# Moving the value-weight loads, the rope tables and the folded output-weight stores of a decoder trunk kernel

## The chip, the cores and the metric

The kernel runs on one core of one Trainium2 chip. The metric is the device time of one execution in microseconds (us). The kernel before has a median of 2416.42 us over 3 runs (2415.17 to 2416.45).

## The reference

One layer of a decoder trunk on 2048 tokens of width 1024, all in fp32, with 256 memory tokens:

```python
h = rmsnorm(x, mix_norm_g)
q, k, v, g, u = split(h @ w_in)                    # 5 x 512 columns
y_ret = silu(g) * head_rmsnorm(retention(q, k, v, positions))   # 4 heads, rotary q and k
y_pool = pool_mixer(u, pool_w, pool_scale)         # 4 groups: window mean minus token, then a 128x128 matrix
x = x + concat([y_ret, y_pool]) @ w_out
x = x + cross_attn(rmsnorm(x), mem_n, xa_wq, xa_wkv, xa_wo)     # 4 heads of 256, memory of 256
x = x + conv_glu_ffn(rmsnorm(x), ...)              # width 2816, causal conv of 3
return rmsnorm(x)
```

## The kernel before, in words

**Arithmetic.** Every fp32 product is done as three matmuls of rounded operands. `split` (lines 256 to 267) makes the two halves of an operand: the high half is an ACT activation (L259, or L262 with a scale per partition), the low half is a DVE subtraction (L243 or L251). `passes` (269 to 273) issues the three matmuls: high by high (L271), high by low (L272), low by high (L273). A matmul therefore first waits for ACT, and its two companions for DVE.

**Tokens.** They go through in two blocks of T = 1024 (b = 0 and 1), each in two stretches of SUB = 512. P is 128, KT is 8 tiles of the model width, HEADS is 4, NMEM is 256.

**Weights folded at the start.** A generator, `folded_weights` (439), runs once and is advanced step by step by `folded(n)` (2010). Its steps in order: keys and values of the memory; for each of four heads the key side is multiplied into the query weight `wqT`, evacuated at L548 and stored to `Md`; then each pooling matrix is multiplied into its rows of the output weight, evacuated at L592 and stored to `WPd` (L594); then for each head and each half of the columns, a "half item", the memory values are multiplied into `wo`, evacuated at L633 and stored to `VWd` (L634). There are eight half items. A loop over n (2021 to 2036) advances this generator once per n and interleaves token loads. At n = 16 to 19 it also calls `value_weights` (730), which loads 512 KB of `w_v` and splits it; this stands ahead of the step of the generator, so that the load is issued ahead of the rows of `wqT` that the step loads.

**After that,** for each block: `values` (739) multiplies tokens by the split value weights and calls `between` after every half, which advances partial sums of tokens and, from its third call on, the tables of the rotary embedding (`rope_steps`, 1998, which stores them by SP at L2005). Then come the projections of the heads, two steps of the generator, and what is left of the work behind, with one step of the generator after each. Then the output units (L2116 on): for each of 8 tiles of the model width, unit n loads a half of `wout_r` (L2118) and a half of `WPd` (L2119) into one slot, splits both (`pairs`) and multiplies them with the mixed tokens. Between the first units the generator is advanced by (1, 2, 4, 0, ...) steps.

**Places.** Tiles come from fixed arenas: `raws` has five 4 KB places for arriving weights (R three, S two), `prs` places for split pairs (Q, and what other arenas lend), Z eight places of 4 KB for evacuated results, TT for temporaries. A slot that is taken again makes its new writer wait for its last reader; a store that still reads a Z slot holds up the next evacuation into it. PSUM has five banks for matmul results (`mm`), so a sixth result waits until the first was evacuated.

**Order.** The program is put into each engine's queue by a scheduler that follows the order in which the code issues, with a look ahead; where the code says `issue_after` or `keep_in_program_order`, it is bound. On each engine instructions run in that order, so an instruction that waits holds all behind it. SP issues nearly all loads, ACT the stores named above.

## Time and profile before

| what | value |
|---|---|
| median of 3 runs | 2416.42 us |
| profiled execution | 2421.08 us, span 2419.3 us |
| granted clock of PE in it | 0.997 |
| busy: PE, DVE, ACT, POOL | 2390.1, 1734.0, 1350.3, 276.0 us |
| DMA | 511.53 MB, mean 211 GB/s |

The span runs from the first to the last instruction of the core. A row of a timeline gives the start in us, the duration of one instruction (or of a merged group, from first start to last end), the engine, the line and the operation with the names of what it writes and reads; in brackets stands the time that its engine was idle just before it, and what ended that. A matmul of 128x512 is listed with 0.39 us, but the next one starts 0.23 us later, since they overlap. An engine's name with a q (SPq, ACTq) is its issuing of DMAs, whose transfers run on 16 DMA engines. In the rows by stretch, the columns are the stretch, its length, the busy time (and instructions) of PE, its weight loads, DVE, ACT and POOL, the granted clock of PE, the share of time that the DMA engines are busy, and GB/s.

### The profile page before, as it was taken

To read this page: it belongs to the slowest core of one execution; us is meant where nothing else is said; L and a number is where in the kernel's file an instruction comes from. 1 tells how busy PE (TensorE), PEld (TensorE's weight loads), DVE (VectorE), ACT (ScalarE), POOL (GpSimd) and SP (SyncE) were. 2 spreads that over 40 slices of the span, in tenths; PEclk is the share of its full clock that TensorE was granted. 3 is DMA by queue.
4 is the path that set the end of the run, shared out by engine and by line. 5 is a ranking of instruction groups with operands and counts; after the bars stand their busy time and mean duration, and the time that the engine had idled before them with its cause. 6 is when DMAs were issued, how large, how long until landed. Compare 5 with 4: busy or idle time off the path is not lost.

```text
span 2419.3 us, 33286 instructions
## 1 busy us (share of the span) xinstructions
PE 2390.1 (99%) x11186; PEld 1993.0 (82%) x11186; DVE 1734.0 (72%) x2904; ACT 1350.3 (56%) x2488; POOL 276.0 (11%) x437
## 2 busy tenths in 40 slices
PE   9999999999999999999999999999999999999998
PEld 8888878888888888888888888888888888887886
DVE  7787774754667665665789776987677698877876
ACT  7654564443445543434555555755555577676673
POOL 0010000063034444100001000110000000000000
PEclk9999999999999999999999999999999999999999
DMA  9732187499688799785477554765455479757952
GB/s 360 262 122 90 63 269 231 135 255 329 194 231 218 188 244 322 195 283 191 140 243 258 184 190 131 251 194 183 158 175 185 134 257 314 238 178 265 345 180 74
DMA packets 267451, 511.53 MB, mean 211 GB/s; under 512 B 29184, under 2 KB 58384, under 8 KB 267280
## 3 DMA queue, kind: packets, MB, share of 16 engines
q1 hardware_dynamic: 209312, 402.30, 50.1%
q0 software_dynamic: 32768, 77.61, 13.1%
q10 hardware_dynamic: 25200, 29.49, 3.5%
q8 instruction: 88, 1.44, 0.2%
q14 instruction: 83, 0.68, 0.1%
HBM read 397.61 MB, written 180.89 MB: 239 GB/s over the span
## 4 chain that ended last, share of the span: by engine, by line
PE 94%; DMA 2%; ACT 2%; DVE 1%; issue 0%; SPq 0%; ACTq 0%; DVEq 0%
PE mm L271 29%; PE mm L272 29%; PE mm L273 29%; PE aux L271 1%; PE aux L273 1%; PE aux L272 1%; ACT G L259 1%; PE aux L901 1%; DMA WPd<-Z 1%; PE aux L778 1%; DVE Z L243 1%; PE aux L806 1%; PE aux L790 0%; PE aux L808 0%; DMA R<-wkv 0%
## 5 line engine op out<-in xcount | busy, mean ns | idle before, releaser
L271 PE MATMUL mm<-G,Q 128*128 128x512 f32 (+1 forms) x1631 | 624.7, 384 | 6.9 <-ACT Q L259 2.7
L273 PE MATMUL mm<-G,Q 128*128 128x512 f32 (+1 forms) x1631 | 619.8, 383 | 0.8 <-DVE Q L243 0.8
L272 PE MATMUL mm<-G,Q 128*128 128x512 f32 (+1 forms) x1503 | 574.1, 382 | 0.2 <-DVE G L251 0.2
L272 PE MATMUL mm<-G,E 128*128 128x512 f32 (+1 forms) x1092 | 420.7, 385 | 0.0
L271 PE MATMUL mm<-G,E 128*128 128x512 f32 (+1 forms) x1092 | 419.2, 386 | 0.5 <-ACT E L259 0.5
L273 PE MATMUL mm<-G,E 128*128 128x512 f32 (+1 forms) x1092 | 418.4, 385 | 0.4 <-DVE E L243 0.4
L271 PEld LDWEIGHTS mm<-G,Q 128*128 128x128 f32 x1631 | 307.0, 188 | 69.2 <-ACT Q L259 4.0
L273 PEld LDWEIGHTS mm<-G,Q 128*128 128x128 f32 x1631 | 306.8, 188 | 60.6 <-DVE Q L243 1.8
L272 PEld LDWEIGHTS mm<-G,Q 128*128 128x128 f32 x1503 | 283.0, 188 | 53.5 <-DVE G L251 0.4
L243 DVE TENSOR_TENSOR Z<-Z,mm 128x512 f32<-128x512 f32 (+1 forms) x322 | 216.4, 676 | 124.6 <-PE mm L273 121.8
L251 DVE SCALAR_TENSOR_TENSOR Z<-Z,vecs 128x1024 f32<-128x1024 f32 x176 | 224.9, 1282 | 50.3 <-ACT Z L1134 48.0
L271 PEld LDWEIGHTS mm<-G,E 128*128 128x128 f32 x1092 | 205.3, 188 | 41.8 <-ACT E L259 0.7
L273 PEld LDWEIGHTS mm<-G,E 128*128 128x128 f32 x1092 | 205.3, 188 | 41.8 <-DVE E L243 0.7
L272 PEld LDWEIGHTS mm<-G,E 128*128 128x128 f32 x1092 | 205.3, 188 | 41.0
L1071 ACT ACTIVATE E<-R 128x512 fp32r<-128x512 f32 (+1 forms) x165 | 101.6, 616 | 146.9 <-PE mm L272 138.7
L243 DVE TENSOR_TENSOR Q<-R,Q 128x512 fp32r<-128x512 f32 x174 | 119.0, 688 | 53.0 <-ACT Q L259 34.7
L243 DVE TENSOR_TENSOR T<-T 128x512 f32<-128x512 f32 (+4 forms) x189 | 130.0, 692 | 23.4 <-ACT T L432 12.0
L243 DVE TENSOR_TENSOR G<-T,G 128x512 fp32r<-128x512 f32 (+1 forms) x173 | 113.8, 678 | 32.4 <-ACT G L1018 18.9
L1018 ACT ACTIVATE G<-T 128x512 fp32r<-128x512 f32 x186 | 111.8, 623 | 36.5 <-DMA T<-Gd 28.6
L1134 ACT ACTIVATE Z<-Z,vecs 128x1024 f32<-128x1024 f32 x88 | 109.2, 1242 | 31.8 <-DVE Z L243 30.8
L1071 ACT ACTIVATE E<-S 128x512 fp32r<-128x512 f32 (+1 forms) x107 | 65.9, 616 | 108.8 <-PE mm L272 106.9
L243 DVE TENSOR_TENSOR E<-R,E 128x512 fp32r<-128x512 f32 (+1 forms) x133 | 89.3, 675 | 43.8 <-ACT E L1071 43.1
(348 smaller groups left out, 3948.3 us busy)
## 6 DMA issues: line engine op xcount, KB each, us to landing
T<-Gd SPq DMA_DIRECT2D x173, 256.0 KB, 4.3
Ud<-w_up POOLq DMA_DIRECT2D x132, 256.0 KB, 9.1
Gd<-Z SPq DMA_DIRECT2D x110, 256.0 KB, 2.6
R<-Ud SPq DMA_DIRECT2D x106, 256.0 KB, 2.8
R<-w_up SPq DMA_DIRECT2D x80, 256.0 KB, 3.1
S<-Ud SPq DMA_DIRECT2D x70, 256.0 KB, 2.9
Gd<-T SPq DMA_DIRECT2D x56, 256.0 KB, 3.3
S<-w_up SPq DMA_DIRECT2D x52, 256.0 KB, 3.1
```

Source lines behind the costliest of these rows:

```text
L243: return eng.tensor_tensor(out=out, in0=a, in1=b, op=op)
L251: return dve.scalar_tensor_tensor(out=out, in0=a, scalar=s, in1=b, op0=op0, op1=op1)
L259: one = act.activation(hi, src, AF.Copy)
L271: pe.matmul(ps, lh, rh, start=start, stop=False, skip_group_check=more)
L272: pe.matmul(ps, lh, rl, start=False, stop=False, skip_group_check=more)
L273: latest[0] = pe.matmul(ps, ll, rh, start=False, stop=stop, skip_group_check=more)
L778: pe.matmul(col(sc, c), self.ch(k, c), self.ch(q, c), start=True, stop=True)
L806: pe.matmul(col(y, c), col(self.pr.f, c), self.ch(v, c, h * T), start=True, stop=self.cur[c] is None)
L901: pe.transpose(tp[:, j * P : (j + 1) * P], e.f[:, j * P : (j + 1) * P], ident)
L1018: one = act.activation(hi, x, AF.Copy, scale=-1.0 if i == 2 else 1.0)
L1071: act.activation(p2[:, 0, :w], self.raw[i].f[:, :w], AF.Copy)
L1134: act.activation(self.c[g].f, a[:, 2:], AF.Identity, bias=cb[:, f : f + 1], scale=cw[2][:, f : f + 1])
```

## The change

There are six edits, on the parts named above.

1. In the loop over n, `value_weights` moves behind `folded(1)` and one n later: part 0 at n = 17, part 1 at 18, parts 2 and 3 at 19.
2. The tables of the rotary embedding for block 0 begin earlier: five steps at the end of that loop, then one in every call of `between`. Their stores in block 0 go by ACT, not SP.
3. `WPd`: groups 0 and 1 each take one Z place and free it at once, groups 2 and 3 share a place of two. The evacuations write in the order (tile, group, column), and the store of groups 2 and 3 is one DMA of 1 MB whose runs are 1 KB long. So there are 3 stores and not 4.
4. `VWd`: the two halves of a half item are stored by one DMA of 512 KB with runs of 1 KB, so 8 stores and not 16. The evacuations write with a stride.
5. Before the first output unit, two steps of the generator and not one are done for each step of the work behind, and between the units (2, 2, 2, 0, ...) rather than (1, 2, 4, 0, ...). So three half items precede the first unit.
6. Output units: `unit_weights` loads `wout_r` and `WPd` of unit n + 1 before unit n is computed, and holds its place meanwhile.

```diff
-        vp4, held = G[:, 8 * T : 12 * T].rearrange("p (n i m) -> p n i m", i=2, m=NMEM), []
-        ended = []
+        vp4, ended = G[:, 8 * T : 12 * T].rearrange("p (n i m) -> p n i m", i=2, m=NMEM), []
         for g in range(4):
             u = ahead.pop(0)
-            if g < 2:
-                held.append(Z.take())
-            t = held[g % 2]
+            if g < 3:
+                held = Z.take(1 + g // 2)
+                t = held.f.rearrange("p (n k c) -> p n k c", n=KT, c=P)
...
-                done = act.activation(t.f[:, nh * SUB : (nh + 1) * SUB], ps, AF.Copy)
+                done = act.activation(t[:, 4 * nh : 4 * nh + 4, g % (held.n)], ps.rearrange("p (n c) -> p n c", c=P), AF.Copy)
             ended.append(done)
-            act.dma_start(WPd[:, :, g, :].rearrange("n p c -> p n c"), t.f.rearrange("p (n c) -> p n c", n=KT))
-            if g > 1:
-                t.free()
+            if g != 2:
+                act.dma_start(WPd[:, :, g + 1 - held.n : g + 1, :].rearrange("n p k c -> p n k c"), t)
+                held.free()
...
-                out = t.f[:, mt * SUB : (mt + 1) * SUB]
-                ended.append(act.activation(out, ps, AF.Identity, scale=rn[:, mt : mt + 1]))
-                act.dma_start(tiles4(VWd, nh, 2 * h + mt), out.rearrange("p (n c) -> p n c", n=4))
+                out = t.f.rearrange("p (n k c) -> p n k c", n=4, c=P)
+                ended.append(act.activation(out[:, :, mt], ps.rearrange("p (n c) -> p n c", c=P), AF.Identity, scale=rn[:, mt : mt + 1]))
+            act.dma_start(VWd[4 * nh : 4 * nh + 4, :, 2 * h : 2 * h + 2, :].rearrange("n p k c -> p n k c"), out)
...
-            sp.dma_start(rope_d[b][i], r.f[:, :SUB])
+            (sp if b else act).dma_start(rope_d[b][i], r.f[:, :SUB])
...
+    tables = rope_steps(0)
     for n in range(1, 2 * KT + HEADS):
...
-        if 2 * KT <= n < 2 * KT + 4:
-            wv.append(value_weights(n - 2 * KT, B.arenas[(n - 2 * KT) // 2]))
         folded(1)
+        for kp in {2 * KT + 1: (0,), 2 * KT + 2: (1,), 2 * KT + 3: (2, 3)}.get(n, ()):
+            wv.append(value_weights(kp, B.arenas[kp // 2]))
+    for _ in range(5):
+        next(tables)
...
-        tables = iter(()) if b else rope_steps(0)
+        tables = iter(()) if b else tables
...
-            if place[0] > 2:
-                next(tables, None)
+            next(tables, None)
...
             folded(2)
             for _ in behind[0]:
-                folded(1)
+                folded(2)
...
+        def unit_weights(n):
+            r = raws.take()
+            sp.dma_start(r.f[:, :SUB], wout_r[n].rearrange("p k c -> p (k c)"))
+            fetched[0] = sp.dma_start(r.f[:, SUB:], WPd[n].rearrange("p k c -> p (k c)"))
+            return r
+
+        soon = unit_weights(first)
         for n in range(first, KT):
-            raw = new_raw()
-            sp.dma_start(raw[:, :SUB], wout_r[n].rearrange("p k c -> p (k c)"))
-            fetched[0] = sp.dma_start(raw[:, SUB:], WPd[n].rearrange("p k c -> p (k c)"))
+            raw, soon = soon, unit_weights(n + 1) if n + 1 < KT else None
+            w = pairs(raw.f)
+            raw.free()
...
-            unit(raw, mixed, add_residual(b, n, xs, got=got), (0, 1, 2, 4, 6, 7, 5, 3) if b == 0 else range(KT))
+            unit(w, mixed, add_residual(b, n, xs, got=got), (0, 1, 2, 4, 6, 7, 5, 3) if b == 0 else range(KT))
...
-                folded((1, 2, 4, 0, 0, 0, 0, 0)[n])
+                folded((2, 2, 2, 0, 0, 0, 0, 0)[n])
```

SP's queue, the loads of the folded query heads and of the value weights, before (L497 loads rows of `wqT`, two for each head, L732 a part of `w_v`, L658 tokens):

```order
L732 DMA R<-w_v 128x2x512
L497 DMA R<-wqT 128x1024
L497 DMA S_78<-wqT 128x1024
L658 DMA Z_74<-xT 128x1024
L732 DMA S_79<-w_v 128x2x512
L497 DMA R<-wqT 128x1024
L732 DMA R<-w_v 128x2x512
L497 DMA R<-wqT 128x1024
L497 DMA S_78<-wqT 128x1024
L497 DMA S_79<-wqT 128x1024
```

and now, at the same place (lines are one less from there on: L731 is `w_v`, L657 the tokens):

```order
L497 DMA R<-wqT 128x1024 x2
L657 DMA Z_74<-xT 128x1024
L497 DMA S_78<-wqT 128x1024
L497 DMA S_79<-wqT 128x1024
L731 DMA R<-w_v 128x2x512
L497 DMA R<-wqT 128x1024 x2
L731 DMA S_78<-w_v 128x2x512
L497 DMA S_79<-wqT 128x1024
L497 DMA R<-wqT 128x1024
L731 DMA R<-w_v 128x2x512 x2
```

The rows of the first two heads now stand ahead of all value weights, and two of the four parts stand behind the last rows.

ACT's queue ahead of the first output unit, before (L633 evacuates a half item, L634 stores it; the `Q<-R` row is the first split of unit 0's `WPd` half):

```order
L816 ACTIVATE T<-aux_2832,sm_2682 128x128 x4
L816 ACTIVATE T<-aux_2844,sm_2682 128x128 x4
L634 DMA VWd<-Z_74 128x4x128
L633 ACTIVATE Z_74<-mm_3027,rnm 128x512
L259 ACTIVATE G<-S_2951 128x512
L259 ACTIVATE G<-S_79 128x512
L634 DMA VWd<-Z_74 128x4x128 x2
L259 ACTIVATE G<-Z_74 128x512
L259 ACTIVATE Q<-R 128x512
L259 ACTIVATE G<-R 128x512
L259 ACTIVATE E_2946<-Z_74 128x512
L633 ACTIVATE Z_74<-mm_3124,rnm 128x512
```

and now (L632 evacuates, L633 stores; `mm_3039` and `mm_3047` are the third half item; of the two `G<-R` the first splits unit 0's `wout_r` half, the second its `WPd` half):

```order
L815 ACTIVATE T<-aux_2844,sm_2682 128x128 x4
L632 ACTIVATE Z_74<-mm_3016,rnm 128x4x128
L632 ACTIVATE Z_74<-mm_3024,rnm 128x4x128
L259 ACTIVATE G<-S_2951 128x512
L259 ACTIVATE G<-S_79 128x512
L633 DMA VWd<-Z_74 128x4x256
L259 ACTIVATE G<-Z_74 128x512
L259 ACTIVATE G<-R 128x512 x2
L632 ACTIVATE Z_74<-mm_3039,rnm 128x4x128
L632 ACTIVATE Z_74<-mm_3047,rnm 128x4x128
L259 ACTIVATE Q<-R 128x512 x2
L633 DMA VWd<-Z_74 128x4x256
```

In both, evacuations stand behind the split of unit 0's `WPd` half; now they are those of the third half item, which on PE comes before unit 0.

PE's queue there, now (`mm_3079` and `mm_3080` are unit 0's two banks, `mm_3144` and `mm_3152` those of the fourth half item):

```order
L820 MATMUL aux_3056<-consts,T 128x128 x4
L271 MATMUL mm_3079<-G 128x512
L272 MATMUL mm_3079<-G 128x512
L271 MATMUL mm_3080<-G 128x512
L272 MATMUL mm_3080<-G 128x512
L271 MATMUL mm_3144<-G 128x512
L272 MATMUL mm_3144<-G 128x512
L273 MATMUL mm_3144<-G 128x512
L271 MATMUL mm_3144<-G 128x512
L272 MATMUL mm_3144<-G 128x512
L273 MATMUL mm_3144<-G 128x512
L271 MATMUL mm_3152<-G 128x512
```

Four matmuls of unit 0 and the six of a bank of the fourth half item follow the third half item; `mm_3152` then takes the bank that `mm_3039` leaves.

## The prediction

> **What bounds the kernel now.** I read the page's busy times first, then the waits of the tensor engine, then the timelines of PE, ACT and the SP queue in the two stretches that the change rewrites.
>
> ```profile
> span 2419.3 us, 33286 instructions
> PE 2390.1 (99%) x11186; PEld 1993.0 (82%) x11186; DVE 1734.0 (72%) x2904; ACT 1350.3 (56%) x2488; POOL 276.0 (11%) x437
> ```
>
> PE is busy for 2390.1 of 2419.3 us: about 29 us are idle, and the change removes no matmul. So it can win only part of those 29 us, and lose by adding to them. The waits of PE name where they lie:
>
> ```profile
> PE mm L271 <- ACT G L259: 3.4, 2, 2.2
> PE mm L271 <- ACT Q L259: 2.7, 3, 1.3
> PE mm L271 <- ACT Z L592: 0.6, 1, 0.6
> PE mm L271 <- ACT Z L633: 0.6, 1, 0.6
> ```
>
> The first row is stretch A (folded query heads, 64 to 70 us). The others lie, but for 0.7 us of the second, in stretch C (folded output weights, 327 to 348 us). All the rest of the order on PE is the same in both kernels but for swaps of neighbours, so I cost A and C and give the remainder nothing.
>
> **Part A: value weights behind the query rows.** Timeline of PE, then of ACT, then of the SP queue:
>
> ```profile
> 64.29 0.28 PE L273 MATMUL mm<-G 128*128 128x256 f32 x1
> 66.72 0.38 PE L271 MATMUL mm<-G 128*128 128x256 f32 x1 [2.15 <-ACT G L259]
> 69.84 0.39 PE L271 MATMUL mm<-G 128*128 128x256 f32 x1 [1.28 <-ACT G L259]
> 86.07 0.40 PE L271 MATMUL mm<-G 128*128 128x512 f32 x1
> 66.00 0.67 ACT L259 ACTIVATE G<-R 128x512 fp32r<-128x512 f32 x1
> 67.04 0.68 ACT L259 ACTIVATE E<-R 128x512 fp32r<-128x512 f32 x1
> 67.56 1.19 ACT L262 ACTIVATE G<-Z,vecs 128x1024 fp32r<-128x1024 f32 x1
> 68.61 0.66 ACT L259 ACTIVATE E<-R 128x512 fp32r<-128x512 f32 x1
> 69.12 0.66 ACT L259 ACTIVATE G<-R 128x512 fp32r<-128x512 f32 x1
> 59.40 0.38 SPq L732 DMA_DIRECT2D R<-w_v  x1
> 60.00 0.33 SPq L497 DMA_DIRECT2D R<-wqT  x1
> ```
>
> PE stands for 2.15 us and again for 1.28 us, 3.43 in all, until ACT has split the second head's rows into their high halves. Ahead of that head's second split (69.12) ACT does a value-weight split (67.04 and 68.61) and a token piece (67.56), and the row itself was asked for only at 60.00, behind a value-weight load (59.40). The change asks for the query rows first and splits them among the evacuations of the head before, as the order of ACT has it: the slots and the places in SP's queue that value weights had go to them, so they can land while the head before is still being multiplied. The value weights come later, where they have cover: nothing uses the first of them before 86.07, and the last two are needed 24 matmuls after that, 24 x 0.23 = 5.5 us (0.23 is the step from one such matmul to the next, as from 326.70 to 326.93 below).
>
> Does ACT have the room? The stretch by engine (length, then PE, weight loads, DVE, ACT, POOL, granted clock, DMA share, GB/s):
>
> ```profile
> 60.00:86.00 26.00, 22.57 (x183) 21.96 (x182) 15.21 (x22) 22.87 (x50) 0.00 (x0) 1.00 0.98 340
> 86.00:150.00 64.00, 63.74 (x282) 52.49 (x282) 52.49 (x91) 30.80 (x52) 4.54 (x8) 1.00 0.51 171
> ```
>
> ACT is busy 22.87 of the 26 us to 86, and the split work is the same in another order: ACT could at best end 3.1 us earlier, and PE (22.57 busy) 3.4. What could stay is a wait of some 0.5 us where an evacuation now stands behind a split of 0.51 (a split's step, as from 68.61 to 69.12). I take 3.1 won. The DMA share of 0.98 is the danger: loads cannot be faster, only in a better order. The bounds are 2.0 (one of the two waits stays in part) and 3.9.
>
> **The rope tables.** Five steps move beside the last folded head, and their stores go from SP to ACT. They end a chain that PE waits on once:
>
> ```profile
> 149.53 0.50 PE L271 MATMUL mm<-G,Q 128*128 128x512 f32 x1 [0.26 <-DVE T L243]
> 137.18 4.12 DMA Z<-rope
> 147.67 1.82 DVE T L243 x3
> ```
>
> The tables then come some 10 us earlier, and the 0.26 goes: with its start-up about 0.3 us. The stores cost ACT as many issues, beside an ACT that is busy 30.80 of 64 us there; on SP the loads behind them lose what stood ahead. DVE, 52.49 of 64, has room for the tables earlier. So nothing is later for it. Part A together: 3.1 + 0.3 = **3.4 us won**, bounds 2.0 and 4.2.
>
> **Part C: the folded output weights and the first output unit.** The chain of waits (first four), PE's timeline and ACT's:
>
> ```profile
> 313.04 4.26 DMA R<-wout_p
> 327.90 7.24 DMA WPd<-Z
> 336.28 5.61 DMA WPd<-Z
> 341.98 5.39 DMA R<-WPd
> 326.70 0.39 PE L272 MATMUL mm<-G 128*128 128x512 f32 x1
> 326.93 0.39 PE L273 MATMUL mm<-G 128*128 128x512 f32 x1
> 336.82 0.50 PE L271 MATMUL mm<-G,Q 128*128 128x512 f32 x1 [1.28 <-ACT Q L259]
> 339.01 0.80 PE L271 MATMUL mm<-G 128*128 128x512 f32 x1 [0.59 <-ACT Z L633]
> 348.07 0.49 PE L271 MATMUL mm<-G,Q 128*128 128x512 f32 x1 [0.69 <-ACT Q L259]
> 335.16 0.60 ACT L592 ACTIVATE Z<-mm 128x512 f32<-128x512 f32 x1 [1.59 <-DMA WPd<-Z]
> 347.39 0.63 ACT L259 ACTIVATE Q<-R 128x512 fp32r<-128x512 f32 x1 [4.23 <-DMA R<-WPd]
> 348.97 1.24 ACT L633 ACTIVATE Z<-mm,rnm 128x512 f32<-128x512 f32 x2
> 335.24:338.65 3.41, 1.91 (x7) 0.86 (x5) 3.41 (x9) 3.41 (x7) 0.00 (x0) 1.00 0.99 343
> 338.65:342.06 3.41, 3.05 (x10) 2.58 (x11) 3.20 (x6) 3.41 (x12) 0.00 (x0) 0.50 1.16 343
> VWd<-Z ACTq DMA_DIRECT2D x6, 256.0 KB, 5.1
> WPd<-Z ACTq DMA_DIRECT2D x4, 512.0 KB, 7.2
> ```
>
> How before runs: the last store of WPd leaves at 336.28 and lands 5.61 later; the load of unit 0's WPd half takes 5.39; ACT waits 4.23 for it, splits it, and PE goes on at 348.07. Whatever PE does until then is ordered by that chain, so its earlier waits, and the half clock of 338.65 to 342.06 (granted 0.50, so 3.41/2 = 1.7 us of work lost), cost nothing extra: they are covered. In those 21 us PE has done 54 matmuls of 0.23 us of half items and of unit 0 (24 for items 0 and 1, 18 for unit 0, 12 for item 2), counted in its order, and 8 transposes.
>
> After: groups 2 and 3 share one slot pair and one store of 1 MB, which saves the wait of 1.59 us for a held slot. Replaying ACT's new order with the durations above puts that store at about 334.65, 1.6 earlier than 336.28. How long a 1 MB store takes no row shows. From below: 5.61, as the 512 KB store. From above: the step from 256 KB (5.1) to 512 KB (7.2) is 2.1, and two more such steps give 11.4. The stretch moves 343 GB/s with a DMA share of 0.99, and 512 KB more at that rate are 1.53 us, so I take 5.61 + 1.53 = 7.15. It lands at 341.8, hardly before the 341.89 of now, the load of 5.39 lands at 347.3.
>
> What differs is what stands behind the wait. ACT's new order has the split of unit 0's WPd half ahead of item 2's evacuations (L632), and PE's next accumulator, the second of item 3, waits for such an evacuation. So PE can do items 0 to 2 (36), 4 matmuls of unit 0 and 6 of item 3: 46 and the 8 transposes, then it stands. My replay starts item 0 at 330.5; 46 x 0.23 are 10.6, the transposes and short waits for splits (the longest, 1.25, for a low half from DVE) 3.8: 344.9. It goes on after the split (0.52) and one evacuation (0.6): 347.3 + 1.15 = 348.45. Eight matmuls fewer are done by then, 8 x 0.23 = 1.84. So C costs 348.45 + 1.84 - 348.07 = **2.2 us**.
>
> To this comes the clock. PE then stands for 3.5 us at a stretch. The window of 3.41 us with 1.91 busy, above, was followed by one at half clock; a hole of 3.5 leaves some window about as empty or emptier, and what follows is now uncovered: **1.7 us**. One other window, in stretch A, was as empty and brought nothing:
>
> ```profile
> 65.59:69.00 3.41, 1.83 (x12) 1.59 (x12) 2.11 (x4) 3.41 (x7) 0.00 (x0) 1.00 1.01 354
> 69.00:72.42 3.42, 2.58 (x19) 2.43 (x20) 3.42 (x6) 2.86 (x6) 0.00 (x0) 1.00 1.03 335
> ```
>
> So the drop is likely, not certain. The Trainium skill (TensorE: Matmul & The Clock Gate, HAM oscillation) gives as an abstract rule that PE should have no idle gap over about 3.4 us, the length of the gate's free-running window. The row at 335.24 speaks against it as a bound: gaps of 1.28 and 0.59 us were enough. By the rule a hole of 3.5 us would seldom blank a whole window and C would be 1.7 less.
>
> C together: 2.2 + 1.7 = 3.9 us lost. Bounds: below, no stall at all (first rival), -1.3; above, the 11.4 us store, 8.1. The single VWd stores (8 for 16) save ACT eight issues behind evacuations that nobody waits for; unit weights a unit ahead change only units 1 to 7, before which PE shows no wait now, so both stand at nothing; if the extra raw slot that is held were missing, a half item's load would come later, under the same stall.
>
> The Trainium skill (DMA: Bandwidth & Descriptors, Measured) lists 6.15 us for a load of 1 MB issued from GpSimd and advises batching to 1 MiB; by it the store would land 1 us sooner and C would be 1 us less. No run here shows that figure.
>
> **The rivals.** *First, faster: no stall.* The store leaves 1.6 us earlier than replayed, takes 5.61, and the load takes 4.26 as R<-wout_p did when the queues were less full: PE could go on at 348.45 - 1.6 - 1.54 - 1.13 = 344.2, before it stalls. Then C is 344.9 + 1.84 - 348.07 = -1.3, or down to -3.8 if waits such as the 0.6, 1.28 and 0.59 before 340 go also. With A at -3.4: 2416.42 - 4.7 to 2416.42 - 7.2, so 2411.7 to 2409.2, in the middle 2410.5. For it: larger packets, one store fewer, one DMA wait fewer. Against: a DMA share of 0.99 to 1.16 in the stretch.
>
> *Second, slower: the 1 MB store holds up unit 0.* At 11.4 us it lands at 346.05, the load at 351.5, PE goes on at 352.7: C is 6.4 + 1.7 = 8.1; as the same full DMA holds back A (2.0 won), 2422.5. It decides from a store of about 10 us on. For it: the store is the last of the chain and all 16 engines are taken. Against: bytes in all are the same.
>
> *Third, part A does not arrive.* DMA share 0.98 and ACT 22.87 of 26 are the bound, the values wait for their own weights instead, and only C stays: 2420.3. Against it: ACT's 3.1 us of room.
>
> *Fourth, the stall comes but the clock holds,* as at 69.00: 2416.9 - 1.7 = 2415.2.
>
> **How the numbers follow.** The profiled execution took 2421.08 us (span 2419.3); the median of the runs is 2416.42, 4.7 less, and I put the differences on the median. Forecast: 2416.42 - 3.4 + 3.9 = 2416.9, chance 0.38. Rivals: first 0.20, second 0.16, third 0.12, fourth 0.14. A measurement of this kernel can tell 0.2%, 4.8 us, from no change: faster is below 2411.6, slower above 2421.3. Faster is the first rival, 0.20, whose range lies under that line but for its edge; slower the second, 0.16; the rest, 0.64, lies within. The range runs from 2410.3, which leaves the better half of the first rival out, to 2421.5, which leaves out most of the second: together some 0.2.
>
> **What would show it.** A is right if the two waits on ACT G L259 at 64 to 70 are gone or under 0.5 each and the first 128x512 matmul of the values starts at about 82.7 (86.07 now). C is right if PE shows one wait of 2.5 to 4.5 us on ACT Z L632 at 341 to 346 (3.4 earlier by A), ACT a wait on R<-WPd of some 4 us just before, the 1 MB store takes 6.5 to 8 us, and a window at half clock follows. It is wrong if the store lands within 5.6 us or leaves before 330 and PE shows no wait on L632, or if the values begin after 85.

## The result, and the profile after

The changed kernel took 2425.04 us (median of 6 runs, 2422.39 to 2426.97), the kernel before 2416.27 us (6 runs, 2415.17 to 2418.44). The ratio is 1.0035, with a 95% interval of 1.0022 to 1.0048: 8.8 us slower. The forecast was 2416.9; the time is 8.1 us above it and lies above the range. The profiled execution took 2426.88 us. First its page:

```profile
span 2425.1 us, 33280 instructions
PE 2392.6 (99%) x11186; PEld 1994.4 (82%) x11186; DVE 1735.8 (72%) x2904; ACT 1349.9 (56%) x2488; POOL 278.4 (11%) x437
```

PE's busy time grew by 2.5 us with the same 11186 matmuls; the rest of the 5.8 us between the two spans, 3.3 us, is idle time. The waits of PE (us in total, times, longest) name three places:

```profile
PE mm L271 <- ACT Q L259: 3.9, 2, 3.6
PE mm L271 <- DVE T L243: 2.9, 2, 1.5
PE mm L271 <- ACT Z L632: 2.9, 1, 2.9
```

All three are new or longer. The row of stretch A (`<- ACT G L259`), 3.4 us before, is down to 0.4, and its two waits (0.17 and 0.27) now lie at 337.00 and 381.27: in stretch A itself no wait of PE is left. PE's timeline tells when (in brackets the wait, and what ended it):

```profile
81.72 0.40 PE L271 MATMUL mm<-G 128*128 128x512 f32 x1
139.40 0.50 PE L273 MATMUL mm<-G,Q 128*128 128x512 f32 x1 [0.94 <-DVE Q L243]
145.51 0.50 PE L273 MATMUL mm<-G,S 128*128 128x512 f32 x1 [0.33 <-DVE S L243]
150.03 0.50 PE L271 MATMUL mm<-G,Q 128*128 128x512 f32 x1 [1.50 <-DVE T L243]
348.73 0.50 PE L271 MATMUL mm<-G 128*128 128x512 f32 x1 [2.86 <-ACT Z L632]
905.27 0.50 PE L271 MATMUL mm<-G,Q 128*128 128x512 f32 x1 [3.63 <-ACT Q L259]
```

Waits alone don't say what a place cost, since a wait can be covered. So I compare the start of the PE instruction with the same number, counted from the first (the order on PE is the same in both but near 84 to 87, 179 and 337 to 345 us), in the two profiled executions: the kernel minus before, in us, called the lead (negative is ahead). Each mark is a place by before's own time.

| kernel | 97 | 154 | 320 | 381 | 823 | 905 |
|---|---|---|---|---|---|---|
| changed | -2.64 | +0.45 | +0.46 | +4.42 | +4.42 | +9.97 |

- **A** was won (2.64 us ahead at 97) and lost again by 154, in the three waits from 139 to 150: 2.77 of the 3.09 us.
- **C** cost 4.42 - 0.46 = 4.0 us, between 320 and 381.
- **D**, a place that the prediction does not speak of, cost 9.97 - 4.42 = 5.5 us near 901, in the second block's output units.

After that nothing more is lost. The lead of 9.97 is more than the 8.8 us of the medians and more than the 5.8 us between the two profiled executions, because before's own profiled execution lost some 4.3 us near 2206. Its windows there (length; PE, weight loads, DVE, ACT, POOL busy; granted clock; DMA share; GB/s):

```profile
2205.75:2209.16 3.41, 1.57 (x6) 1.10 (x7) 3.34 (x10) 3.37 (x8) 0.00 (x0) 1.00 0.41 131
2209.16:2212.57 3.41, 3.41 (x10) 2.63 (x9) 3.41 (x7) 1.50 (x3) 0.00 (x0) 0.50 0.24 64
```

A window in which PE was busy for 1.57 of 3.41 us was followed by one at half clock. Every other kernel's execution, set against it, gains 2.7 to 4.3 us at that place, the changed kernel's 4.3. It accounts for most of the 4.8 us by which before's profiled 2421.08 lies above its median; the marks therefore end at 905.

**Place A, 87 to 150 us.** SP's queue, DVE and the chain of waits in the changed kernel:

```profile
126.67 3.58 SPq L1610 DMA_DIRECT2D Z<-rope  x3
130.36 0.56 SPq L1064 DMA_DIRECT2D S<-w_qkgu  x1
```

```profile
87.28 0.49 DVE L247 TENSOR_SCALAR T<-T,consts 128x512 f32<-128x512 int32 x1 [3.51 <-DMA T<-pos]
95.86 0.69 DVE L243 TENSOR_TENSOR S<-S 128x512 f32<-128x512 f32 x1 [1.32 <-ACT T L1563]
136.85 1.29 DVE L243 TENSOR_TENSOR Z<-Z,T 128x512 f32<-128x512 f32 x2 [2.38 <-DMA Z<-rope]
144.16 0.69 DVE L243 TENSOR_TENSOR R<-R 128x512 f32<-128x512 f32 x1 [2.41 <-DMA R<-w_qkgu]
```

In before the first of those sums ran at 88.29:

```profile
88.29 0.69 DVE L243 TENSOR_TENSOR S<-S 128x512 f32<-128x512 f32 x1 [6.95 <-ACT T L1564]
```

DVE now does table work from 87.28 on, and the sums behind it begin 7.6 us later (95.86 for 88.29). On SP the reads of the tables (Z<-rope) now stand ahead of a weight load (130.36). At 136.85 DVE waits 2.38 us for a table read. Its next steps (138.06, 138.66) free the place that the next weight load takes, so this load is issued only at 139.38, and DVE waits 2.41 us for it; its landing is in the chain below.

**Places C and D.** Pieces of the chain of waits (start, length), ACT's timeline, and windows:

```profile
139.38 4.69 DMA R<-w_qkgu
334.79 7.29 DMA WPd<-Z
342.13 5.31 DMA R<-WPd
895.59 8.09 DMA T<-xT
```

```profile
347.47 0.63 ACT L259 ACTIVATE G<-R 128x512 fp32r<-128x512 f32 x1 [4.22 <-DMA R<-WPd]
903.70 0.33 ACTq L864 DMA_DIRECT2D Xd<-T  x1
904.07 0.60 ACT L427 ACTIVATE aux<-T 128x512 f32<-128x512 f32 x1 [3.76 <-DMA T<-xT]
904.61 0.61 ACT L259 ACTIVATE Q<-R 128x512 fp32r<-128x512 f32 x1
```

```profile
349.60:353.00 3.40, 3.40 (x10) 2.63 (x9) 3.10 (x5) 3.40 (x8) 0.00 (x0) 0.51 1.03 396
895.60:903.70 8.10, 6.04 (x27) 4.68 (x25) 4.92 (x8) 2.60 (x5) 5.12 (x8) 1.00 1.03 374
906.00:909.40 3.40, 3.40 (x10) 2.67 (x9) 1.88 (x3) 1.12 (x2) 1.37 (x3) 0.50 1.10 280
```

C is the forecast chain: the 1 MB store leaves at 334.79 and takes 7.29, the load takes 5.31, ACT waits 4.22, PE 2.86, and a half-clock window follows. D has the same shape from another cause. ACT issues a store of output tokens to `Xd` (L864) only at 903.70, when a load that it has no data from, T<-xT, issued by SP at 895.59, has landed 8.09 us later. The split Q<-R at 904.61, which PE needs, stands behind that store. In the built program each DMA of SP and ACT waits for the completion of the one eight before it in their common order (eight completion semaphores, used in turn); the load of 895.59 and the store of 903.70 have the same semaphore, with seven other DMAs between them. Before has the same kind of wait, but there it hurts nobody:

```profile
894.28 0.61 ACT L259 ACTIVATE Q<-R 128x512 fp32r<-128x512 f32 x1
900.82 0.33 ACTq L865 DMA_DIRECT2D Xd<-T  x1
901.19 0.60 ACT L427 ACTIVATE aux<-T 128x512 f32<-128x512 f32 x1 [2.77 <-DMA S<-wout_r]
```

Its split of 894.28 stands ahead of the store that waits, and PE shows no wait near 901.

### The profile page after: what moved, and what is told of

Read it like the earlier page. It is cut to its first block, busy times and chain, and to the rows that moved or that the text cites. A ratio compares the mean times of both kernels' runs of the same rounds, so it can differ in the third digit from the quotient of the medians.

```text
span 2425.1 us, 33280 instructions
## 1 busy us (share of the span) xinstructions
PE 2392.6 (99%) x11186; PEld 1994.4 (82%) x11186; DVE 1735.8 (72%) x2904; ACT 1349.9 (56%) x2488; POOL 278.4 (11%) x437
## 4 chain that ended last, share of the span: by engine, by line
PE 95%; DMA 2%; ACT 1%; DVE 1%; issue 0%; SPq 0%; ACTq 0%; DVEq 0%
PE mm L271 30%; PE mm L272 30%; PE mm L273 30%; PE aux L271 1%; PE aux L273 1%; PE aux L272 1%; PE aux L900 1%; DVE Z L243 1%; DMA WPd<-Z 1%; PE aux L777 1%; PE aux L805 1%; PE aux L789 0%; PE aux L807 0%; ACT G L259 0%; PE aux L363 0%; DMA T<-xT 0%
```

## The experiments

The numbers of the edits are those of the change. The medians of before beside them were 2415.92, 2416.26, 2415.63 and 2416.28 us in the four groups, each on one chip; below are the median, the ratio with its 95% interval, and the lead at the marks.

| kernel | us | ratio | 97 | 154 | 320 | 381 | 823 | 905 |
|---|---|---|---|---|---|---|---|---|
| values_only | 2420.56 | 1.0018 (1.0010 to 1.0027) | -2.89 | +0.24 | +4.84 | +3.76 | +4.77 | +4.77 |
| tables_only | 2415.97 | 1.0001 (0.9993 to 1.0010) | +1.96 | +1.76 | +1.76 | +0.58 | +0.60 | +0.60 |
| no_tables | 2426.14 | 1.0042 (1.0029 to 1.0056) | -2.03 | +1.25 | +5.55 | +4.99 | +4.99 | +9.36 |
| tail_only | 2421.60 | 1.0025 (1.0015 to 1.0036) | +0.20 | -0.02 | -0.07 | -2.96 | -2.96 | +1.42 |
| split_behind | 2421.52 | 1.0023 (1.0013 to 1.0032) | -3.00 | -1.01 | +0.02 | -0.67 | -0.64 | +3.36 |
| old_units_b1 | 2423.41 | 1.0025 (1.0015 to 1.0034) | -3.04 | +0.67 | +0.61 | +0.84 | +0.87 | +7.03 |
| tail_old_b1 | 2423.15 | 1.0025 (1.0016 to 1.0034) | +0.04 | +0.84 | +0.80 | -0.79 | -0.76 | +5.53 |
| fewer_steps | 2413.78 | 0.9989 (0.9980 to 0.9997) | -3.12 | -2.14 | -2.18 | -4.70 | -4.72 | -4.72 |
| one_dma_more | 2419.04 | 1.0012 (1.0003 to 1.0021) | -2.58 | -0.07 | +0.92 | +1.68 | +1.68 | +2.54 |
| old_items | 2414.64 | 0.9994 (0.9985 to 1.0003) | -3.30 | -0.82 | -0.66 | -2.32 | -2.30 | -2.32 |
| items_only | 2423.84 | 1.0029 (1.0019 to 1.0040) | +2.43 | +1.83 | +1.71 | +1.31 | +1.29 | +6.08 |
| joined | 2416.06 | 1.0000 (0.9991 to 1.0009) | -3.02 | -3.39 | -3.32 | -1.35 | -1.30 | -0.45 |
| both_mended | 2418.49 | 1.0009 (1.0000 to 1.0018) | -2.28 | +0.62 | +0.62 | +0.04 | +0.04 | +0.90 |
| old_items_few | 2413.01 | 0.9988 (0.9979 to 0.9997) | -3.59 | -3.19 | -3.23 | -4.43 | -4.41 | -4.39 |
| few_units | 2413.48 | 0.9988 (0.9979 to 0.9997) | -3.58 | -3.37 | -3.45 | -6.69 | -6.49 | -6.49 |

Each mark comes from one execution, and at C two executions of one order differ by 3.8 us (below), so a mark is read for several kernels together, beside their medians. The medians have a spread too: two of the rows turn out to repeat the instructions of another kernel (under place D), and each pair is 1.2 to 1.6 us apart.

### Which edit gives back part A

My theory after the result was that the early tables (edit 2) gave the lead back; the rival, that it is lost by the values themselves. **values_only** makes edit 1 alone, **tables_only** edit 2 alone, **no_tables** all but edit 2.

```diff
-        if 2 * KT <= n < 2 * KT + 4:
-            wv.append(value_weights(n - 2 * KT, B.arenas[(n - 2 * KT) // 2]))
         folded(1)
+        for kp in {2 * KT + 1: (0,), 2 * KT + 2: (1,), 2 * KT + 3: (2, 3)}.get(n, ()):
+            wv.append(value_weights(kp, B.arenas[kp // 2]))
```

> The kernel before with the first edit alone (value weights behind the query rows). Theory, the tables on DVE gave part A back: both waits on ACT G L259 at 64 to 70 us go, the values begin about 2 to 3.5 us earlier than 86.07 and the gain stays to 155 us, since the quarter sums are still first on DVE; about 2413.0 us. Rival, the values' own loads and splits hold them, or the later token loads make the quarter sums late whatever DVE does: the lead at 155 us is under 1 us, about 2416.

```diff
-            sp.dma_start(rope_d[b][i], r.f[:, :SUB])
+            (sp if b else act).dma_start(rope_d[b][i], r.f[:, :SUB])
...
+    tables = rope_steps(0)
...
+    for _ in range(5):
+        next(tables)
...
-        tables = iter(()) if b else rope_steps(0)
+        tables = iter(()) if b else tables
...
-            if place[0] > 2:
-                next(tables, None)
+            next(tables, None)
```

> The kernel before with the second edit alone (rope tables early, their stores by ACT). Theory: DVE does the tables ahead of the quarter sums, the query and key sums come later, and PE waits on DVE at 138 to 150 us for 2 to 4 us more than before; about 2418 to 2420. Rival, what was lost there came from the moved loads of the first edit: no new wait at 138 to 150 us, and the 0.26 us wait at 149 is gone; about 2416.

and for **no_tables** the same lines taken out of the changed kernel:

```diff
-    for _ in range(5):
-        next(tables)
...
-        tables = iter(()) if b else tables
+        tables = iter(()) if b else rope_steps(0)
...
```

> The changed kernel without the second edit (tables as before). In its order on ACT the evacuations of the third half item stand ahead of the split of unit 0's WPd half. Theory: the 3.8 us won at 70 us stay (lead at 155 us 3 or more), the wait on ACT Z L632 of 2.9 us and the half clock after it are gone or under 1 us; what is left over is the new wait near 901 us, if it is there; about 2411 to 2413, or 2416 to 2418 with that wait. Rival, the stall before unit 0 is set by the landing of WPd whatever stands behind the split: PE waits 2.5 us or more there, about 2417 to 2420.

My theory fell. Tables alone cost nothing (1.0001); values_only, without the early tables, is 4.6 us slower than before; and no_tables, for which 2411 to 2418 was expected, came out at 2426.14, no faster than the changed kernel. values_only gains 2.89 by 97 and loses 3.13 of it by 154. PE in values_only:

```profile
145.51 0.50 PE L273 MATMUL mm<-G,S 128*128 128x512 f32 x1 [1.86 <-DVE S L243]
149.81 0.50 PE L271 MATMUL mm<-G,Q 128*128 128x512 f32 x1 [1.29 <-DVE T L243]
252.96 0.50 PE L271 MATMUL mm<-G,Q 128*128 128x512 f32 x1 [1.25 <-ACT Q L1708]
```

The chain there has the old tables as its cause:

```profile
137.57 5.97 DMA Z<-rope
```

PE comes 3 us earlier, the tables land at 143.54 where before had them at 141.30 (137.18 + 4.12), and PE waits 3.15 us in the first two rows. It goes on losing 4.6 us from 154 to 320: 1.25 in the last row, 1.96 in a wait for ACT that ends at 299.44, and a half clock from 300.7 to 307.5. no_tables loses 4.3 there as well, with the same two waits (1.24 and 1.96), and every kernel with both edits 1 and 2 at most 1.0 there. So the tables have to come earlier if the values do, and edit 2 is no burden by itself. What remained was that five steps at once put other work on DVE late. **fewer_steps** makes edits 1 and 2 on the kernel before with two steps:

```diff
...
+    for _ in range(2):
+        next(tables)
...
```

> The first and second edits alone, but with two steps of the tables ahead of the values and not five. Theory, each order of the early work on DVE leaves one transfer late at 138 to 150 us, the round trip of the tables or the loads of w_qkgu, and two steps lie between: the lead of 4 us at 74 us is 0.5 to 2.5 us at 155 us; about 2413.5 to 2416. Rival, the first edit's lead is lost there whatever the tables do, since the loads behind it are later: lead under 0.3 us, 2416 or above.

It is 2.5 us faster than before. At 154 the lead is still 2.14, and PE has one wait left in that place:

```profile
147.43 0.50 PE L271 MATMUL mm<-G,Q 128*128 128x512 f32 x1 [1.28 <-DVE T L243]
```

SP in fewer_steps, to be set beside 130.36 above:

```profile
125.34 0.33 SPq L1065 DMA_DIRECT2D S<-w_qkgu  x1
129.97 0.64 SPq L1611 DMA_DIRECT2D Z<-rope  x1
```

The weight load is issued 5 us earlier, ahead of the table reads. The four kernels with both edits and two steps (fewer_steps, joined, old_items_few, few_units) keep 2.1 to 3.4 us at 154; the six with both edits and five steps (changed, split_behind, old_units_b1, one_dma_more, both_mended, old_items) are between -1.0 and +0.7. That the number of steps decides is shown. How it does is read from the traces alone. It is not the late start of the sums, for in fewer_steps the first of them is as late:

```profile
95.39 0.69 DVE L243 TENSOR_TENSOR S<-S 128x512 f32<-128x512 f32 x1 [2.93 <-ACT T L1564]
137.14 2.49 DVE L243 TENSOR_TENSOR Z<-Z,T 128x512 f32<-128x512 f32 x4
```

The second row shows another difference. With two steps DVE takes the tables up behind the step that frees the place for the next weight load, and without a wait, and that load is issued at 137.26 and not at 139.38; with five, table work stands ahead of that step and waits 2.38 us for a read. No run separates this from the places in SP's queue.

### What place C is

Theory: unit 0's split stands ahead of the third half item's evacuations on ACT. Rival: the 1 MB store is late, wherever the split stands. **tail_only** undoes edits 1 and 2 in the changed kernel and keeps the rest:

```diff
-        for kp in {2 * KT + 1: (0,), 2 * KT + 2: (1,), 2 * KT + 3: (2, 3)}.get(n, ()):
-            wv.append(value_weights(kp, B.arenas[kp // 2]))
-    for _ in range(5):
-        next(tables)
...
```

> The changed kernel without the first and second edits, so the folded output weights, the three half items and the unit weights alone. In its order on ACT one evacuation of the third half item stands ahead of the split of unit 0's WPd half, the other behind. Theory: the start up to 155 us is as in before (both waits of 2.15 and 1.28 there), the stall before unit 0 is shorter than 2.9 us but may come one accumulator later; about 2417 to 2419 without the wait near 901 us, 5 us more with it. Rival, the stall is set by the landing: 2.9 us and half clock as in the changed kernel, 2420 or more.

Here C wins 2.9 us instead of losing 4.0, with edits 3 to 6 all in place: in its order on ACT one evacuation of the third item stands ahead of the split. ACT waits 4.04 us for the load there too (345.15), but PE shows no wait behind it. In no_tables both evacuations stand ahead of the split, and C wins 0.6.

**split_behind** binds that order in the changed kernel; beside it only a few neighbours change places, from 341 to 421 us:

```diff
             evacuated.append(ended[-1])
...
-            w = pairs(raw.f)
+            with tc.issue_after(evacuated[-1].ins) if not b and n == 0 else nullcontext():
+                w = pairs(raw.f)
```

> The changed kernel with one bond more: the splits of unit 0's weights are bound behind the last evacuation of the third half item on ACT. Theory, PE stalls because that evacuation stands behind a split that waits for WPd: the wait on ACT Z L632 of 2.9 us at 345 goes or is under 0.7 us, no half clock at 350, and the 4.0 us that this stretch costs become 0 or a gain; about 2420 to 2421.5 with the start and the wait near 901 us as they are. Rival, the landing of WPd sets it and PE would stall a little later for unit 0 itself: a wait of 1.5 us or more on a split of unit 0, about 2424.

The median falls by 3.5 us against the changed kernel (2421.52 for 2425.04), and by 1.9 against old_units_b1 (2423.41), which runs the same instructions as the changed kernel and was measured beside it. C goes from +4.0 to -0.7. ACT, then PE, in split_behind:

```profile
341.17 1.25 ACT L634 ACTIVATE Z<-mm,rnm 128x512 f32<-128x512 f32 x2
344.83 0.63 ACT L259 ACTIVATE G<-R 128x512 fp32r<-128x512 f32 x1 [1.89 <-DMA R<-WPd]
```

```profile
342.99 0.50 PE L271 MATMUL mm<-G 128*128 128x512 f32 x1 [1.26 <-ACT G L259]
```

The two evacuations (341.17) now stand ahead of the split (344.83). ACT still waits for the load, but no accumulator waits behind it. So the order on ACT is the cause, and the load only its length. How much it costs varies: **old_units_b1** (below) has the changed kernel's order, and in its execution:

```profile
341.35 4.12 DMA R<-WPd
```

```profile
346.75 0.50 PE L271 MATMUL mm<-G 128*128 128x512 f32 x1 [0.23 <-ACT Z L632]
```

The load took 4.12 for 5.31 and PE waited 0.23 for 2.86: C cost 0.2 there and 4.0 in the changed kernel. In one_dma_more, also of this order, PE waited 0.89, and C cost 0.8. In both the clock was halved ahead of the stall (from 340.5 and 340.7), where the wait for the load covers what is lost; in the changed kernel behind it (from 349.6), where nothing does. So the forecast stall and nearly none both occur, in different executions of one order. The second is not the prediction's first rival, for the store took some 7 us there too (issued at 334.28, the load behind it at 341.35).

### What place D is

Theory: edit 6 in the second block, which loads a unit ahead, moves the stores behind other loads. Rivals: the number of DMAs before (edits 3 and 4), or edit 5, whose three half items leave the raw places in another rotation. **old_units_b1** and **tail_old_b1** load the second block's units as before, in the changed kernel and in tail_only:

```diff
-        soon = unit_weights(first)
+        soon = None if b else unit_weights(first)
...
+            if b:
+                raw = new_raw()
+                sp.dma_start(raw[:, :SUB], wout_r[n].rearrange("p k c -> p (k c)"))
+                fetched[0] = sp.dma_start(raw[:, SUB:], WPd[n].rearrange("p k c -> p (k c)"))
...
```

> The changed kernel, but in the second block the units load their weights as before (a unit ahead only in the first block). Theory, the 3.6 us wait near 901 us comes from the sixth edit, which moves the splits of a unit's weights on ACT behind a store that waits for a token load: it goes, and with it the half clock after it, 5.5 us; about 2419.5. Rival, the wait comes from the number of DMAs before it (edits three and four), whatever the units do: it stays, about 2425.

> Edits three to six without one and two, and in the second block the units load as before. Theory: the 3.5 us won at 326 to 350 us by edits three to five without the first two stay, the wait near 894 us and its half clock (4.4 us) are gone; about 2412.5 to 2414, which is faster than the kernel before and than the changed one. Rival, the loss near 894 us stays: 2417 to 2421.

D stays: 7.03 - 0.87 = 6.2 and 5.53 + 0.76 = 6.3 us. The traces say why: on every engine, in all instructions and DMA issues with their semaphores, old_units_b1 runs the order of the changed kernel, and tail_old_b1 that of tail_only. In that block edit 6 moves nothing, so it is not the cause, and this theory fell. The two runs are thus repeats: beside its own before, the changed kernel is 8.8 us slower and old_units_b1 7.2, tail_only 5.7 and tail_old_b1 6.9. A difference of some 1.6 us between two medians here can't be told from none. **old_items** undoes edit 5 in the changed kernel, **items_only** makes edit 5 alone on the kernel before:

```diff
-                folded(2)
+                folded(1)
...
-                folded((2, 2, 2, 0, 0, 0, 0, 0)[n])
+                folded((1, 2, 4, 0, 0, 0, 0, 0)[n])
```

> The changed kernel without the fifth edit (two half items ahead of unit 0, and 1, 2, 4 between the units). In its program the Xd store near 901 us waits for another DMA, as in the kernel before. Theory, the fifth edit alone brings both losses, the stall ahead of unit 0 (the third item's evacuation behind the split) and the one near 901 us: no wait of over 1 us at either place; about 2415 to 2417. Rival, the other edits carry a share: 2419 or more.

> The kernel before with the fifth edit alone. Theory: the stall near 896 us is there, 2.5 us or more and a half clock after it, 4 to 6 us together; at 326 to 350 us, where the evacuations of the third item stand ahead of the split, it wins 0 to 2 us; about 2418.5 to 2421. Rival, the 901 us stall needs the other edits: about 2415.

Edit 5 brings D: without it the lead does not move between 823 and 905 (-2.30 and -2.32), with it alone it moves by 4.8 us, and items_only, which has neither edit 3 nor edit 4, is 8.2 us slower than before, nearly as much as the whole change. That is more than D: 2.43 us of it were lost by 97 in its profiled execution, in the order of before, with the clock halved from 68.7 to 75.5, and whether its other executions have this is not known. C is gone without edit 5 as well (old_items wins 1.7 there), but edit 5 alone does not bring it (items_only wins 0.4). PE in items_only:

```profile
901.40 0.65 PE L271 MATMUL mm<-G,Q 128*128 128x512 f32 x1 [2.88 <-ACT Q L259]
```

All seven kernels with edit 5, but for those with the next edit, lose 4.0 to 6.3 us from 823 to 905; the six without edit 5 lose nothing there. **one_dma_more** tests the wait itself. It loads a piece of tokens in two halves, so that every later DMA has another DMA eight before it. In the trace this load comes twice, near 487 and near 879 us, so there are two DMAs more by D (1425 on SP for 1423) and not one, with the same bytes. From 862 to 915 us the order on PE, ACT and DVE is that of the changed kernel:

```diff
-            fetched[0] = sp.dma_start(out[s].f[:, :SUB], xT[...])
+            for c in ((0, SUB // 2), (SUB // 2, SUB)) if (b, k, s) == (1, 0, 0) else ((0, SUB),):
+                fetched[0] = sp.dma_start(out[s].f[:, c[0] : c[1]], xT[...])
```

> The changed kernel, with the first token load of the second block's output units (256 KB) issued as two halves, so one DMA more and the same bytes. In the program each DMA of SP and ACT waits for the completion of the one eight before it (eight completion semaphores go round); with the extra DMA the Xd store near 901 us follows an earlier Xd store and no longer a token load. Theory, that wait on ACT, with a split of the next unit's weights behind it, is the stall near 901 us: PE's 3.6 us there go to under 0.5, and the half clock with them, 5 us; about 2420. Rival, the split itself is late for its own load or for a place: PE still waits 2 us or more there, about 2425.

Beside its own before it is 3.4 us slower, where the changed kernel is 8.8 and old_units_b1 7.2: 3.7 to 5.4 us come back. D costs 2.54 - 1.68 = 0.9 instead of 5.5. ACT, then PE, in one_dma_more:

```profile
896.95 0.33 ACTq L865 DMA_DIRECT2D Xd<-T  x1
898.77 0.63 ACT L259 ACTIVATE Q<-R 128x512 fp32r<-128x512 f32 x1 [0.71 <-PE aux L272]
902.89 0.60 ACT L427 ACTIVATE aux<-T 128x512 f32<-128x512 f32 x1 [2.60 <-DMA S<-wout_r]
```

```profile
899.46 0.50 PE L271 MATMUL mm<-G,Q 128*128 128x512 f32 x1 [0.55 <-ACT Q L259]
```

The store ahead of the split now leaves at once, the split runs at 898.77, and the long wait falls to the next store (902.89), behind which nothing is urgent, as in before. Two DMAs more, and so more work, make the kernel faster: the store waited for the wrong load. How edit 5, far away in the first block, comes to move the order here is read from the order alone (the places for raw weights are handed out in another rotation, and the units' loads and splits in the second block are ordered by them); no run tested it.

### Whether the mended parts add up

**both_mended** is the changed kernel with split_behind and one_dma_more; **joined** has the two steps of fewer_steps as well:

```diff
-    for _ in range(5):
+    for _ in range(2):
         next(tables)
```

> The changed kernel with unit 0's splits bound behind the third item's evacuations and the first token load of the second block's units in two halves; five steps of the tables ahead as in the change. Theory, the two losses add and are all: 2425 - 3.5 - 6 = 2415.5, level with the kernel before within 1.5 us. Rival, they overlap (one stall moves into the other): 2418 or more.

> The changed kernel with three mends: two steps of the tables ahead of the values and not five, unit 0's splits bound behind the third item's evacuations, and the first token load of the second block's units in two halves. Theory, the three losses are separate and add: lead at 155 us of 1.5 to 2.5, at 352 us of 2 to 5, kept to the end; about 2411 to 2413.5, faster than both kernels. Rival, a gain that is won early is lost at the next front that DMA sets: 2415 to 2417.

Each beside its own before, both_mended is 6.6 us faster than the changed kernel, where split_behind (3.5) and one_dma_more (5.4) sum to 8.9; against old_units_b1 it is 4.9, where they sum to 1.9 + 3.7 = 5.6. So that it falls short of the sum is not shown. In its execution C is -0.6, D 0.9, and A still lost, as it has five steps; 2.2 us above before remain. joined, at 2416.06, fell on the side of its rival: it has its full lead of 3.3 us at 320 and loses 2.0 of it from 320 to 381. PE there:

```profile
324.41 0.51 PE L271 MATMUL mm<-G 128*128 128x512 f32 x1 [1.08 <-ACT Z L593]
336.76 0.79 PE L272 MATMUL mm<-G 128*128 128x512 f32 x1 [1.27 <-DVE G L243]
```

These waits come ahead of the split, and a half-clock window follows them (from 336.8). They don't come from the lead alone: few_units (below), with a lead of 3.45 at 320 and without edits 3 to 5, wins another 3.2 by 381 at full clock. The first of them stands in old_items_few too (1.05 at 324.46), which has edits 3 and 4 but not 5; the last does not. Which edit brings which was not tested alone.

**old_items_few** is the changed kernel without edit 5 and with two steps; **few_units** is the kernel before with edits 1, 2 (two steps) and 6:

```diff
-    for _ in range(5):
+    for _ in range(2):
         next(tables)
...
-                folded(2)
+                folded(1)
```

> The changed kernel without the fifth edit and with two steps of the tables ahead of the values and not five. Theory: the lead of 3 us or so at 155 us is kept through the output units, no stall near 901 us; 2411 to 2413, faster than both kernels. Rival, the landing of WPd fixes the first output unit in time whatever came before: 2414 to 2416.

> The first, second (two steps ahead) and sixth edits, without the grouped stores and the third half item. Theory, as in the run with the first two edits and two steps: 2412.5 to 2414.5. Rival, the grouped stores are what wins at 326 to 350 us and without them the lead is lost there: 2415 or more.

With fewer_steps they are the three that beat both kernels: 2413.0, 2413.5 and 2413.8 us, 2.5 to 3.3 below before, with intervals just short of one. That is under the 0.2% that the prediction took as the bound. What edits 3, 4 and 6 add to edits 1 and 2 with two steps is at most 0.8 us between these medians, and can't be told from nothing.

## Why the prediction was wrong

**A, the waits at 64 to 70: right.** They fell from 3.4 us to none, and the lead at 97 was 2.64 (3.1 forecast, bounds 2.0 and 3.9). The first 128x512 matmul of the values started at 81.72 (82.7 forecast), but seven of these now stand ahead of the last matmuls of the heads, so the lead is the fairer measure.

**A, the tables: the first step that failed.** "DVE, 52.49 of 64, has room for the tables earlier. So nothing is later for it." DVE had the room as a share, but not in order. "The tables then come some 10 us earlier" was mis-sized too: the last read had landed at about 136.8, where before had it at 141.30, and DVE waited 2.38 us for it, ahead of the step that frees the next weight load's place. The lead of 2.64 turned into +0.45 by 154. With two steps and not five 2.1 to 3.4 us of the lead are kept, so the number of steps is the cause; by which of the delays stays open. It was worth asking what the first user after the values waits for: with tables as before, a PE that comes 3 us earlier only waits 3.15 us for them (values_only), where before waited 0.26. The third rival, "part A does not arrive", held for A in its result and not in its cause: it named the DMA share and the values' own weights, and it was the work behind the values.

**C: right in mechanism, and in size by luck.** Forecast 3.9, measured 4.0: the store at 334.79 (334.65 forecast) took 7.29 (7.15), the load 5.31 (5.39), PE stood from about 345.9 to 348.73 (344.9 to 348.45), and the half-clock window came. split_behind shows that the order on ACT is what counts. But in two other executions of the same order it cost 0.2 and 0.8, as the half clock came ahead of the stall, so that the profiled one came so near to 3.9 was luck within 0 to 4. The Trainium skill (DMA: Bandwidth & Descriptors, Measured) has 6.15 us for a load of 1 MB; the store here took 7.29, at a DMA share of 0.94. The measurement decides, and the sum from the rows was nearer.

**The rest: the step that failed worst.** "All the rest of the order on PE is the same in both kernels but for swaps of neighbours, so I cost A and C and give the remainder nothing." The order on PE was the same there, but D lies in the order on ACT and in which DMA is eight before which. It cost 5.5 us at 901, and edit 5 brought it. "Both stand at nothing" held for edits 4 and 6, as far as the runs tell: old_items_few has both (0.9988), few_units edit 6 without edit 4 (0.9988).

The sum of the lead at 905: A 3.4 forecast won, 0.45 lost: 3.85. C 0.06. D 5.55. Together 9.5, which is the difference between +9.97 and the forecast of +0.5. On the medians it is 8.1, or 1.4 less: the changed kernel's profiled execution is 1.8 above its median, before's without its 4.3 only 0.5 above its own.

## What to carry to other kernels

A busy share below 1 says that an engine has room, not that the moved work falls into it: follow the first user of what stands behind the moved work in each queue, and the first wait that an earlier engine will then meet. Where DMAs share a few completion semaphores in turn, adding or removing a transfer changes which transfer each later one waits for; look at every instruction that stands behind a DMA issue on an engine that the bottleneck waits for, in all later stages too. And a split that waits for a load is dear ahead of an evacuation that could have gone first: bind the order of the two. Before reading an experiment, compare the order that it runs with the order of the kernel that it alters: two of the runs here altered nothing.

## What the runs showed of the hardware

- Half-clock windows follow stretches with far less than a window of idle time, and not always. In one_dma_more:

```profile
337.30:340.70 3.40, 2.09 (x9) 1.33 (x9) 3.40 (x8) 3.40 (x12) 0.00 (x0) 1.00 1.06 373
340.70:344.10 3.40, 3.40 (x12) 2.60 (x11) 3.40 (x7) 1.80 (x4) 0.00 (x0) 0.50 1.01 336
```

  PE was busy for 2.09 of 3.40 us and still lost half of the next window. The Trainium skill (TensorE: Matmul & The Clock Gate, HAM oscillation) gives the abstract rule of no idle gap over about 3.4 us. It agrees with D (3.63, then half clock) and not with C (2.86, then half clock), nor with these rows; the measurement decides.
- The same order can fall either way. tables_only has before's order on every engine here, where before ran on at full clock after a window with 1.83 us busy:

```profile
65.40:68.80 3.40, 1.90 (x12) 1.59 (x12) 2.00 (x4) 3.40 (x7) 0.00 (x0) 0.92 1.05 376
68.80:72.20 3.40, 2.45 (x11) 2.45 (x12) 3.40 (x5) 2.97 (x6) 0.00 (x0) 0.50 0.93 332
```

  Here the clock fell, and 1.96 us were lost in that execution, which its median does not show (2415.97).
- A token load of 256 KB (T<-xT) took 8.09 us at 895.59, while the DMA share was 1.03 and 374 GB/s were moved: longer than the 1 MB store of 7.29 at 334.79, with a DMA share of 0.94 and 312 GB/s. Which transfers it shared the engines with was not taken apart.
